# Building four sums of gate weights with six transfers from memory and two copies on the chip

## The chip, the cores and the metric

The kernel runs on one core of one Trainium2 chip. A core has a matrix engine (PE, with its weight loads shown as PEld), a vector engine (DVE), a scalar engine (ACT), a general engine (POOL), a queue engine that issues transfers (SP), and 16 DMA engines that move data between the chip's memory (HBM) and the on-chip buffer. Each engine works through its own instructions in the order in which they were scheduled at build time; an instruction that must wait holds up everything behind it on the same engine. The metric is the device time of one execution in microseconds (us). Before the change the median of three executions is 1417.95 us (1417.14 to 1418.25).

## The reference

The program is a two-layer decoder trunk over 512 tokens of width 1024: a token mixer (Mamba-2 in layer 0, HGRN2 in layer 1), a squared-ReLU MLP, two layer norms and a gated per-layer input. The change lies in the last step of the last layer:

```python
h = layer_norm(DEEPNORM_ALPHA * h + sq_relu_mlp(h, mlp_w1[i], mlp_w2[i]), ln_g[i, 1], ln_b[i, 1])
x = h + jax.nn.sigmoid(h @ ple_w_gate[i]) * (p[i] @ ple_w_proj[i])
```

`ple_w_gate` is a 1024 x 1024 matrix in 32-bit floats.

## The kernel before

**Precision.** Every matrix product in 32-bit precision is made of three: each operand is split into a high part `whi` (a cast on ACT, L113) and a low part `wlo` (value minus high part, on DVE, L116), and `mm3` (L120 to L122) multiplies high by high, high by low and low by high. A weight tile is 128 x 1024 numbers, 512 KB. `unit` loads one into a ring of three buffers named `raw` through SP (L106) and splits it; `split` alone splits a tile that is already on the chip. The rings `whi` and `wlo` hold six tiles each. A `raw` buffer can be loaded again only when the `wlo` subtraction has read it.

**Fewer products by sums.** The second MLP matrix and the last gate use a Strassen-like scheme: seven block products instead of eight, which need four sums of weight blocks, t1 to t4. In the MLP `weight_sums` makes them on DVE from loads into tiles tagged `r`, of which there are eight. In the last gate (`last_gate`) they are made by transfers alone: POOL issues eleven transfers from memory, four plain ones that fill the four tiles with block 4 of the gate's weights, then seven that add another block onto a tile as they write it. Each adding transfer waits until the earlier transfer into its tile has landed. The gate's tiles take over `r` buffers of the last group of MLP sums as those are split and released.

**What stands around it.** The last seven products of the MLP run in the order p1, p7, p6, p4, p5, p2, p3. After p5 (tiles `py`) token chunks 0 and 1 of the result `acc` are complete but for their sums of squares, after p3 chunks 2 and 3. For each chunk DVE adds the product from the PSUM bank into `acc` with a running sum (L372), forms the mean (L213), ACT squares (L215), DVE finishes the variance (L218), scales (L223), ACT takes the root (L219), DVE inverts (L221) and scales and shifts once more (L224). PE then turns the chunk by four transposes at a time (L238), ACT and DVE split the turned half (L242, L243), and the gate's products can read it. PE fills the time between the transposes with `proj`, the product of the per-layer input with `wp` (tiles `pj<-whi,a` and so on).

**What sets the order.** The order on each engine is fixed by a scheduler when the program is built, from the order of the code and the priority of blocks (`tc.high_priority`, where `LEAD` is 100 and `SOON` 40). SP issues the loads in one queue: in the stretch that matters the two tiles of p3 (`raw<-in_w`), then `wp` (`raw<-in_wp`), then four tiles of the gate (`raw<-in_wg`), each as soon as one of the three `raw` buffers is free. POOL has its own queue, and both share the 16 DMA engines.

Of the kernel before, what the change touches and what calls it, by code (L numbers as in the profile page):

```python
# [12 lines left out]
ALU = mybir.AluOpType  # L13
PSUM = bass.MemoryType.PSUM

P = 128
# [12 lines left out]
SOON = 40  # L29
# [15 lines left out]
def trunk(ctx: ExitStack, tc, a):  # L45
    nc = tc.nc
# [21 lines left out]
    def mk(p, shape, tag, dt=F32, **kw):  # L68
        return p.tile(list(shape), dt, tag=tag, name=nm(tag), **kw)

    def f32(t):
        return t.bitcast(F32)
# [16 lines left out]
    def tmp(tag, shape, dt=F32):  # L89
        return mk(phase[0], shape, tag, dt, bufs=phase[2].get(tag, 1))  # L90
# [11 lines left out]
    def unit(src, lead=LEAD, after=None):  # L102
        n = src.shape[1]
        with tc.high_priority(offset=lead):
            raw = mk(raws, [P, 1024], "raw")
            nc.sync.dma_start(raw[:, :n], src)  # L106
        return split(raw[:, :n], lead, after)

    def split(f, lead=LEAD, after=None):
        n = f.shape[1]  # L110
        with tc.high_priority(offset=lead):
            hi = mk(whip, [P, 1024], "whi", F32R)
            nc.scalar.copy(hi[:, :n], f)  # L113
            lo = mk(wlop, [P, 1024], "wlo", F32R)
            with behind(after):
                nc.vector.tensor_sub(lo[:, :n], f, f32(hi[:, :n]))  # L116
        return hi, lo
# [110 lines left out]
    def behind(ins):  # L228
        return tc.issue_after(ins.ins) if ins is not None else nullcontext()
# [91 lines left out]

    def weight_sums(w, lead, eng=nc.vector, after=None):

        t = [[None, None] for _ in range(4)]

        def load(i, u, src):
            t[i][u] = tmp("r", [P, 1024])
            nc.sync.dma_start(t[i][u], src)

        with tc.high_priority(offset=lead):  # L330
            for u in range(2):
                load(0, u, w[0][1][u])
                load(2, u, w[1][1][u])
                with behind(after):
                    eng.tensor_sub(t[2][u], t[2][u], t[0][u])
                load(1, u, w[0][0][u])
                with behind(after):
                    eng.tensor_sub(t[0][u], t[0][u], t[1][u])
                    eng.tensor_add(t[1][u], t[2][u], t[1][u])
            for u in range(2):  # L340
                load(3, u, w[1][0][u])
                with behind(after):
                    eng.tensor_sub(t[3][u], t[3][u], t[1][u])
        return t

    def block_product(w, blk, lead, first, after=None, turns=None, sums=None, low=None):

        t1, t2, t3, t4 = weight_sums(w, lead, after=low)  # L350
        seen = set() if first else {(i, j) for i in range(2) for j in range(2)}
        banks = {}
# [43 lines left out]
    def last_gate(wp, wg, h_s, p_s, kept, turned):  # L396

        t3, t1, t2, t4 = (tmp("r", [P, 1024]) for _ in range(4))
        with tc.high_priority(offset=SOON):
            for t in (t3, t1, t2, t4):  # L400
                nc.gpsimd.dma_start(t, wg[4])
            for t, n in ((t3, 5), (t1, 0), (t2, 5), (t4, 5), (t2, 0), (t4, 0), (t4, 1)):
                nc.gpsimd.dma_start(t, wg[n], accum_op=ALU.add)

        pairs = [mk(b8, [P, 2, 4, 256], "b8", F32R) for _ in range(2)]
        cells = [mk(b8, [P, 4, T], "b8") for _ in range(3)] + [tmp("blk", [P, 4, T])]
# [18 lines left out]
        def direct(i, q):  # L425
            return lambda k, u: (h_s.h(2 * q + k, tok(2 * i + u)), h_s.l(2 * q + k, tok(2 * i + u)))
# [5 lines left out]
        def part(ps, x, w, u, start, stop=True):  # L432
            for k in range(2):
                ks = slice(k * 512, (k + 1) * 512)
                mm3(ps, *x(k, u), w[0][:, ks], w[1][:, ks], start and k == 0, stop and k == 1, skip_group_check=True)
# [21 lines left out]
        pu = unit(wp[0])  # L457
        b11, b21 = unit(wg[0]), unit(wg[1])
        us = [unit(wg[2]), unit(wg[3])]
        t3 = split(t3)  # L460
        turns = turned(1)
        for c in range(NCH):
            ps = bank(psj, "pj")
# [5 lines left out]
        for u in range(2):  # L469
            part(x[u], direct(0, 0), b11, u, True)  # L470
            nc.scalar.copy(cell(4 + u), x[u])

        turns = [turned(2), turned(3)]
        for u in range(2):
# [38 lines left out]
        t2, t4, t1 = split(t2), split(t4), split(t1)  # L513
# [38 lines left out]
    def mlp_and_gate(layer, h_s, last):  # L552
# [54 lines left out]
        if last:  # L607
            return last_gate(a[f"wp_{layer}"], a[f"wg_{layer}"], h_s, p_s, kept, turned)
# [57 lines left out]
    def values4(xs, rows, late):  # L666

        w = [[[a["whvg"][4 * j + 2 * i + u] for u in range(2)] for j in range(2)] for i in range(2)]
        t1, t2, t3, t4 = weight_sums(w, VALUE_SUMS, nc.vector)
        a11, a12, a21, a22 = (rows[i][:, j] for i in range(2) for j in range(2))  # L670
        res = [[mk(w4, [P, 2, T], "ab"[i]) for i in range(2)] for _ in range(2)]
# [292 lines left out]
    for j in range(17):  # L964
# [6 lines left out]
        if pend is not None:  # L971
            i = j - 1
# [485 lines left out]
```

## Time and profile before

| | |
|---|---|
| profiled execution, its own time | 1417.95 us |
| span from first to last instruction in it | 1416.2 us |
| the three timed executions | 1417.95, 1417.14, 1418.25 us |
| busy share of the span | PE 99%, DVE 76%, ACT 54%, POOL 1% |
| moved by DMA | 183.26 MB, 129 GB/s on average |
| POOL's transfers for the gate's sums | 11 of 512 KB, issued from 1305.1 to 1341.6 us |
| matrix engine's mean granted clock | 0.998 of full speed |

All places in time below are us from the first instruction of this execution. The 1.75 us between its span and its own time lie outside the instructions. The profile gives, for each instruction, its start, its length and, in brackets, how long its engine had been idle and what ended that; a chain of waits follows the work back from the last instruction; rows of DMA give the queue's packets, megabytes and the share of the 16 engines' time that they took (q0 is POOL's queue, q1 SP's), or one issue with the time until it landed.

### The profile page before, as it was taken

To read this page: it belongs to the slowest core of one execution; us is meant where nothing else is said; L and a number is where in the kernel's file an instruction comes from. 1 tells how busy PE (TensorE), PEld (TensorE's weight loads), DVE (VectorE), ACT (ScalarE), POOL (GpSimd) and SP (SyncE) were. 2 spreads that over 40 slices of the span, in tenths; PEclk is the share of its full clock that TensorE was granted. 3 is DMA by queue.
4 is the path that set the end of the run, shared out by engine and by line. 5 is a ranking of instruction groups with operands and counts; after the bars stand their busy time and mean duration, and the time that the engine had idled before them with its cause. 6 is when DMAs were issued, how large, how long until landed. Compare 5 with 4: busy or idle time off the path is not lost.

```text
span 1416.2 us, 20365 instructions
## 1 busy us (share of the span) xinstructions
PE 1408.1 (99%) x8001; PEld 1170.3 (83%) x8001; DVE 1070.8 (76%) x1778; ACT 764.3 (54%) x1156; POOL 10.3 (1%) x23
## 2 busy tenths in 40 slices
PE   9999999999999999999999999999999999999998
PEld 7888888888988888888888888888888888888877
DVE  7989587698977667687977577677785767766885
ACT  7766465573454444545546547655554454544573
POOL 0000000000000000000000000000000000000100
PEclk9999999999999999999999999999999999999999
DMA  8333333234334443445621422222163444444921
GB/s 312 136 114 120 107 116 120 75 105 157 141 105 149 135 148 137 146 138 174 208 75 49 141 85 73 76 76 91 58 240 113 153 131 143 132 159 152 233 95 60
DMA packets 50831, 183.26 MB, mean 129 GB/s; under 512 B 5680, under 2 KB 6448, under 8 KB 50608
## 3 DMA queue, kind: packets, MB, share of 16 engines
q1 hardware_dynamic: 49152, 176.20, 36.7%
q0 software_dynamic: 1584, 5.77, 1.9%
q8 instruction: 63, 1.03, 0.3%
q14 instruction: 32, 0.26, 0.1%
HBM read 179.78 MB, written 2.16 MB: 128 GB/s over the span
## 4 chain that ended last, share of the span: by engine, by line
PE 96%; DVE 1%; DMA 1%; ACT 1%; issue 0%; ACTq 0%; DVEq 0%
PE pj L120 24%; PE pj L121 24%; PE pj L122 24%; PE py L120 5%; PE py L121 5%; PE py L122 5%; PE py L900 1%; PE pt L238 1%; PE py L1169 1%; PE pm L917 1%; PE pm L865 1%; DVE wlo L116 1%; DMA raw<-in_w 1%; PE py L1295 1%; PE pt L853 0%; PE py L1297 0%
## 5 line engine op out<-in xcount | busy, mean ns | idle before, releaser
L113 ACT CAST whi<-raw 128x1024 fp32r<-128x1024 f32 x218 | 229.0, 1051 | 332.5 <-PE pj L121 242.3
L120 PE MATMUL pj<-b,whi 128*128 128x512 f32 (+1 forms) x990 | 378.7, 383 | 0.0
L122 PE MATMUL pj<-b,wlo 128*128 128x512 f32 (+1 forms) x990 | 376.7, 381 | 0.0
L121 PE MATMUL pj<-b,whi 128*128 128x512 f32 (+1 forms) x990 | 376.6, 381 | 0.0
L116 DVE TENSOR_TENSOR wlo<-raw,whi 128x1024 fp32r<-128x1024 f32 x218 | 265.6, 1222 | 143.6 <-ACT whi L113 140.0
L121 PEld LDWEIGHTS pj<-b,whi 128*128 128x128 f32 x990 | 186.4, 188 | 34.5 <-issue 0.9
L122 PEld LDWEIGHTS pj<-b,wlo 128*128 128x128 f32 x990 | 186.3, 188 | 34.5
L120 PEld LDWEIGHTS pj<-b,whi 128*128 128x128 f32 x990 | 186.2, 188 | 34.2
L122 PE MATMUL pj<-whi,b 128*128 128x512 f32 x520 | 205.0, 394 | 0.0
L120 PE MATMUL pj<-whi,b 128*128 128x512 f32 x508 | 202.1, 398 | 0.0
L121 PE MATMUL pj<-wlo,b 128*128 128x512 f32 x508 | 199.1, 392 | 0.0
L113 ACT CAST whi<-r 128x1024 fp32r<-128x1024 f32 x76 | 80.0, 1054 | 67.7 <-PE pj L122 38.2
L122 PEld LDWEIGHTS pj<-whi,b 128*128 128x128 f32 x520 | 98.3, 189 | 20.4
L120 PEld LDWEIGHTS pj<-whi,b 128*128 128x128 f32 x508 | 95.5, 188 | 19.0 <-ACT b L1316 0.3
L121 PEld LDWEIGHTS pj<-wlo,b 128*128 128x128 f32 x508 | 95.5, 188 | 18.8 <-issue 0.2
L116 DVE TENSOR_TENSOR wlo<-r,whi 128x1024 fp32r<-128x1024 f32 x76 | 92.6, 1221 | 23.3 <-ACT whi L113 22.7
L122 PE MATMUL py<-whi,b 128*128 128x512 f32 x260 | 101.3, 390 | 0.0
L121 PE MATMUL py<-wlo,b 128*128 128x512 f32 x248 | 96.5, 389 | 0.0
L120 PE MATMUL py<-whi,b 128*128 128x512 f32 x248 | 96.4, 390 | 0.0
L122 PEld LDWEIGHTS py<-whi,b 128*128 128x128 f32 x260 | 48.8, 188 | 10.2
L794 DVE SCALAR_TENSOR_TENSOR cv<-pj,cst,cv 128x509 f32<-128x509 f32 (+2 forms) x66 | 48.9, 746 | 10.4 <-ACT cv L791 9.7
L120 PEld LDWEIGHTS py<-whi,b 128*128 128x128 f32 x248 | 46.6, 188 | 10.1 <-DVE sg L658 0.3
(360 smaller groups left out, 1900.7 us busy)
## 6 DMA issues: line engine op xcount, KB each, us to landing
raw<-in_w SPq DMA_DIRECT2D x112, 512.0 KB, 3.4
r<-in_w SPq DMA_DIRECT2D x64, 512.0 KB, 3.5
raw<-in_wssd SPq DMA_DIRECT2D x36, 512.0 KB, 3.8
a<-csd SPq DMA_DIRECT2D x16, 512.0 KB, 4.1
raw<-in_wso SPq DMA_DIRECT2D x16, 512.0 KB, 3.3
raw<-in_whq SPq DMA_DIRECT2D x16, 512.0 KB, 3.4
raw<-in_wg SPq DMA_DIRECT2D x15, 512.0 KB, 3.9
raw<-in_whvg SPq DMA_DIRECT2D x14, 512.0 KB, 3.4
```

The source lines that it names most:

```text
L113: nc.scalar.copy(hi[:, :n], f)
L116: nc.vector.tensor_sub(lo[:, :n], f, f32(hi[:, :n]))
L120: nc.tensor.matmul(out, sh, mh, start=start, stop=False, **kw)
L121: nc.tensor.matmul(out, sh, ml, start=False, stop=False, **kw)
L122: return nc.tensor.matmul(out, sl, mh, start=False, stop=stop, **kw)
L238: nc.tensor.transpose(pt[:, j * P : (j + 1) * P], src[:, k * P : (k + 1) * P], ident)
L794: nc.vector.scalar_tensor_tensor(cv[:, d:], ps[:, : T - d], convw[:, i, k : k + 1], cv[:, d:], ALU.mult, ALU.add)
L865: nc.tensor.matmul(pst_[:, c * P : (c + 1) * P], btok[:, c, :], xw[:, c].rearrange("p h q -> p (h q)"), start=True, stop=True)
L900: mm = nc.tensor.matmul(yds[0][64 * r : 64 * r + 64, sl], xdt[:, 2 * c + r, :], m[:, r, sl], start=True, stop=True)
L917: mm = nc.tensor.matmul(yo[:, c * P : (c + 1) * P], pv[:, c - 1].rearrange("p h q -> p (h q)"), cm[:, c * P : (c + 1) * P], start=True, st ...
L1169: nc.tensor.matmul(pcs[r][bs, at : at + n], kk[r][:, ts], qs, start=True, stop=True)
L1295: nc.tensor.matmul(po[:, sl], scs[r][:, c, :], v(c, r), start=True, stop=c == 0)
```

## The change

In `last_gate` the list of transfers is new. t3 and t1 are filled with block 4 and get one adding transfer each (blocks 5 and 0). t2 is now a copy of the finished t3 from the on-chip buffer to the on-chip buffer, plus one adding transfer (block 0), and t4 a copy of the finished t2, plus one adding transfer (block 1). The split of t3 moves behind the first block product of the gate and gets the lower priority `SOON`. In `weight_sums` the eight tiles are allocated up front, those of t[2] and t[1] first, instead of one by one as they are loaded.

```diff
     def weight_sums(w, lead, eng=nc.vector, after=None):
 
-        t = [[None, None] for _ in range(4)]
+        t = [None] * 4
+        for i in (2, 1, 3, 0):
+            t[i] = [tmp("r", [P, 1024]) for _ in range(2)]
 
         def load(i, u, src):
-            t[i][u] = tmp("r", [P, 1024])
             nc.sync.dma_start(t[i][u], src)
...
         t3, t1, t2, t4 = (tmp("r", [P, 1024]) for _ in range(4))
         with tc.high_priority(offset=SOON):
-            for t in (t3, t1, t2, t4):
-                nc.gpsimd.dma_start(t, wg[4])
-            for t, n in ((t3, 5), (t1, 0), (t2, 5), (t4, 5), (t2, 0), (t4, 0), (t4, 1)):
-                nc.gpsimd.dma_start(t, wg[n], accum_op=ALU.add)
+            nc.gpsimd.dma_start(t3, wg[4])
+            nc.gpsimd.dma_start(t1, wg[4])
+            nc.gpsimd.dma_start(t3, wg[5], accum_op=ALU.add)
+            nc.gpsimd.dma_start(t1, wg[0], accum_op=ALU.add)
+            nc.gpsimd.dma_start(t2, t3)
+            nc.gpsimd.dma_start(t2, wg[0], accum_op=ALU.add)
+            nc.gpsimd.dma_start(t4, t2)
+            nc.gpsimd.dma_start(t4, wg[1], accum_op=ALU.add)
...
         us = [unit(wg[2]), unit(wg[3])]
-        t3 = split(t3)
         turns = turned(1)
...
             part(x[u], direct(0, 0), b11, u, True)
             nc.scalar.copy(cell(4 + u), x[u])
+        t3 = split(t3, SOON)
 
```

POOL, the gate's transfers, before. `r_11783` is t3, `r_11784` t1, `r_11785` t2 and `r_11786` t4; L401 fills, L403 adds.

```order
L401 DMA r_11783<-in_wg 128x1024
L403 DMA r_11783<-in_wg 128x1024
L401 DMA r_11784<-in_wg 128x1024
L401 DMA r_11785<-in_wg 128x1024
L403 DMA r_11784<-in_wg 128x1024
L401 DMA r_11786<-in_wg 128x1024
L403 DMA r_11785<-in_wg 128x1024
L403 DMA r_11786<-in_wg 128x1024
L403 DMA r_11785<-in_wg 128x1024
L403 DMA r_11786<-in_wg 128x1024 x2
```

The same place in the changed program (L404, L406 and L408 add; L405 and L407 copy on the chip).

```order
L401 DMA r_11783<-in_wg 128x1024
L403 DMA r_11783<-in_wg 128x1024
L402 DMA r_11784<-in_wg 128x1024
L405 DMA r_11785<-r_11783 128x1024
L404 DMA r_11784<-in_wg 128x1024
L406 DMA r_11785<-in_wg 128x1024
L407 DMA r_11786<-r_11785 128x1024
L408 DMA r_11786<-in_wg 128x1024
```

Eleven transfers became eight, seven adding ones became four, and from the second row on each link of t3, t2, t4 stands behind the one before.

DVE, the norm's end for chunks 0 and 1 and what follows it, before. `wlo_11832` is the low part of the gate's block 3, `wlo_11836` that of t3; `pt_11726` and `pt_11741` are the two turned halves of chunk 0, `lnmv` the means of chunks 2 and 3.

```order
L224 SCALAR_TENSOR_TENSOR acc_99<-acc_99,lnrs_11658,b_11418 128x1024
L116 TENSOR_TENSOR wlo_11832<-raw_11828,whi_11830 128x1024
L243 TENSOR_TENSOR b_1772_11423<-pt_11726,b_1770_11421 128x4x128
L116 TENSOR_TENSOR wlo_11836<-r_11783,whi_11834 128x1024
L372 ISA acc_99,lnsum_11425<-py_1792_11468,acc_99 128x512
L372 ISA lnsum_11425 128x1
L372 ISA acc_99,lnsum_11425<-py_1793_11469,acc_99 128x512
L372 ISA lnsum_11425 128x1
L243 TENSOR_TENSOR b_1773_11424<-pt_11741,b_1771_11422 128x4x128
L213 TENSOR_SCALAR lnmv_11755<-lnsum_11425 128x1
L213 TENSOR_SCALAR lnmv_11769<-lnsum_11425 128x1
```

The same place in the changed program.

```order
L224 SCALAR_TENSOR_TENSOR acc_99<-acc_99,lnrs_11658,b_11418 128x1024
L116 TENSOR_TENSOR wlo_11829<-raw_11825,whi_11827 128x1024
L243 TENSOR_TENSOR b_1772_11423<-pt_11726,b_1770_11421 128x4x128
L373 ISA acc_99,lnsum_11425<-py_1792_11468,acc_99 128x512
L373 ISA lnsum_11425 128x1
L373 ISA acc_99,lnsum_11425<-py_1793_11469,acc_99 128x512
L373 ISA lnsum_11425 128x1
L213 TENSOR_SCALAR lnmv_11755<-lnsum_11425 128x1
L213 TENSOR_SCALAR lnmv_11769<-lnsum_11425 128x1
L116 TENSOR_TENSOR wlo_11896<-r_11783,whi_11894 128x1024
L243 TENSOR_TENSOR b_1773_11424<-pt_11741,b_1771_11422 128x4x128
```

The low part of t3 stands behind the sums and means of chunks 2 and 3 instead of ahead of them. Ahead of these rows no engine but POOL has another order than before, and SP's order is the same throughout.

## The prediction

> **What bounds the kernel now.** I read the page's busy shares first, then who waited for whom on PE, then the chain of waits in order of time where the longest wait lies, then the DMA view of that stretch.
>
> ```profile
> PE 1408.1 (99%) x8001; PEld 1170.3 (83%) x8001; DVE 1070.8 (76%) x1778; ACT 764.3 (54%) x1156; POOL 10.3 (1%) x23
> PE pt L238 <- DVE acc L224: 2.8, 1, 2.8
> ...
> PE pj L120 <- ACT b L509: 0.2, 1, 0.2
> ```
>
> PE is the bound: the change leaves every matmul as it is, so it can act only on PE's waits and on PE's clock. One wait is large: 2.8 us for the layer norm of chunk 0 (L224). It costs more than its length:
>
> ```profile
> 1344.68 0.39 PE L120 MATMUL py<-whi,blk 128*128 128x512 f32 x1
> ...
> 1349.89 0.39 PE L122 MATMUL py<-whi,blk 128*128 128x512 f32 x1
> 1353.11 1.11 PE L238 MATMUL pt<-cst,acc 128*128 128x128 f32 x4 [2.83 <-DVE acc L224]
> 1353.87 0.77 PE L120 MATMUL pj<-whi,a 128*128 128x512 f32 x1
> ...
> 1359.14 0.40 PE L120 MATMUL pj<-whi,a 128*128 128x512 f32 x1
> 1353.00:1359.20 6.20, 6.09 (x17) 4.92 (x18) 5.33 (x9) 1.18 (x2) 0.00 (x0) 0.51 0.42 147
> 1359.20:1365.40 6.20, 6.20 (x33) 5.07 (x32) 2.98 (x6) 5.21 (x12) 0.00 (x0) 1.00 0.00 0
> ```
>
> After the wait PE runs at a granted clock of 0.51 for 6.2 us, then at 1.00 again. The 13 matmuls that start from 1353.87 to 1359.14 (two chunks of six and one) stand 5.27 / 12 = 0.44 us apart, p3's 24 from 1344.68 to 1349.89 stand 5.21 / 23 = 0.23 apart: 12 x 0.21 = 2.5 us, and about 0.4 for the four transposes ahead of them (0.76 us at the half clock). The wait and its slow clock are worth 2.8 + 2.9 = 5.7 us. The chain says who is late:
>
> ```profile
> 1329.66 7.82 DMA raw<-in_w
> ...
> 1337.57 1.06 ACT whi L113
> ...
> 1338.66 1.23 DVE wlo L116
> ...
> 1340.53 0.23 DVE lnmv L213
> ...
> 1343.82 4.92 DMA raw<-in_wg
> ...
> 1351.85 1.21 DVE acc L224
> ...
> 1353.11 1.11 PE pt L238 x4
> ```
>
> The norm stands on DVE and ACT in line with splits of weight tiles, and those wait for loads. p3's two tiles, issued at 1327.37 and 1329.66, took 7.8 us each, `wp` behind them 9.7:
>
> ```profile
> 1327.37 2.61 SPq L106 DMA_DIRECT2D raw<-in_w  x2
> raw<-in_w SPq DMA_DIRECT2D x1, 512.0 KB, 7.8
> 1330.90 0.33 SPq L106 DMA_DIRECT2D raw<-in_wp  x1
> raw<-in_wp SPq DMA_DIRECT2D x1, 512.0 KB, 9.7
> 1335.32 1.05 ACT L113 CAST whi<-raw 128x1024 fp32r<-128x1024 f32 x1 [5.70 <-DMA raw<-in_w]
> 1336.40 1.23 DVE L116 TENSOR_TENSOR wlo<-raw,whi 128x1024 fp32r<-128x1024 f32 x1 [4.32 <-ACT whi L113]
> 1336.29 0.39 PE L122 MATMUL py<-whi,b 128*128 128x512 f32 x1
> 1339.80 0.68 DVE L372 CUSTOM_DVE_ANT_0 acc<-py,acc 128x512 f32<-128x512 f32 x1
> ```
>
> DVE stood idle for 4.3 us, and so took PE's product for chunk 0 at 1339.80 although PE had begun its last matmul at 1336.29. An ordinary load takes 3.2 us; these were slow because POOL's adding transfers shared the DMA engines:
>
> ```profile
> 1327.00:1349.00 22.00, 22.00 (x99) 18.22 (x98) 15.56 (x27) 10.28 (x16) 2.61 (x3) 1.00 0.95 258
> q0 software_dynamic: 1440, 5.24, 66.0%
> q1 hardware_dynamic: 923, 3.39, 24.2%
> q0 software_dynamic: 144, 0.52, 39.1%
> r<-in_wg POOLq DMA_DIRECT2D x1, 512.0 KB, 3.8
> r<-in_wg POOLq DMA_DIRECT2D x1, 512.0 KB, 5.4
> raw<-in_wg SPq DMA_DIRECT2D x1, 512.0 KB, 3.2
> raw<-in_wg SPq DMA_DIRECT2D x1, 512.0 KB, 4.9
> 1341.61 0.87 POOL L403 DMA_DIRECT2D r<-in_wg  x1 [8.14 <-DMA r<-in_wg]
> ```
>
> From 1327 to 1349 the DMA engines are 0.95 busy. The first two queue rows cover 1309 to 1347.1 (38.1 us), the third 1305 to 1309.2, where POOL's first fill is alone. So a plain transfer of POOL costs 39.1% of 4.2 = 1.6 us of all 16 engines; the ten others took 25.1 us, three of them plain, which leaves (25.1 - 4.9) / 7 = 2.9 us for an adding one. The issue rows: the fill at 1305.13 lands after 3.8 us, the first adding one after 5.4; a load of SP takes 3.2 alone (1355.41) and 4.9 beside an adding transfer (1337.65).
>
> **The change, part by part.** *Transfers.* Three adding transfers go (3 x 2.9 = 8.7 us of the engines), and two fills become copies on the chip. No row shows a copy from chip to chip. Its bounds are the plain fill (1.6 us of the engines, landing after 3.8) and the adding one (2.9; 5.4), which also reads the chip; I take the fill, because like it the copy moves every byte once and computes nothing. By the Trainium skill's formula in "DMA: Bandwidth & Descriptors", section "Anatomy of one DMA" (a fixed 2.0 us and bytes over 436 GB/s), a 512 KB copy would land after an estimated 3.2 us; the sum would be the same.
>
> *When they run.* t3 is filled at 1305.13 as before, lands at 1308.9, its adding transfer at about 1314.6 (1309.26 + 5.4). Behind it stand in line copy, add, copy, add: with a fill's 3.8 and an add's 5.4, and about 2 us for t1's two transfers and a norm load sharing, the copy into t2 lands near 1319.5, t2 is done near 1325.5, the copy into t4 near 1329.5, t4 near 1336. With copies at 5.4 it is 1339. Now the last one is only issued at 1341.61. So when p3's loads are issued (1327.37, 1329.66) they meet one POOL transfer at a time, where now they meet parts of three adding ones. I take 4.5 and 4.9 us for them, by the row with one neighbour; bounds 3.2 (alone) and 7.8 (no gain).
>
> *What follows from the loads.* First tile at 1331.9: high part on ACT, low part on DVE (1.06 and 1.23 us, as in the chain), both done by 1334.3. Second at 1334.6: done by 1336.95. PE's product for chunk 0 is ready by 1336.7 (1336.29 + 0.39), so L372 runs at 1336.95, 2.85 us earlier than now, and the mean at 1337.7. From there to PE's transposes now take 1353.11 - 1340.53 = 12.6 us, nearly all of it work in line on DVE and ACT; if it holds, PE begins them at 1350.3, just after its last matmul of p3 lets go (1349.89 + 0.23 = 1350.12). The links that could break it: `wp` must land by about 1338.6, 2.8 us ahead of its use now (third in SP's line, it now lands at 1330.90 + 9.7 = 1340.6), the gate's third tile, 4.92 us from 1343.82, is issued 2.8 us earlier and meets no POOL transfer, and the high parts wait for PE to free a buffer of the `whi` ring, for the third tile at p2's end, about 1344.9 (p3's first matmul starts at 1344.68). These may add up to 0.8 us; I take 0.4, so a rest of about 0.5 us of the 2.8.
>
> *Clock.* With a rest of 0.5 us I take the clock to stay at 1.00, since the wait of 0.2 us at L509 leaves it there; 2.9 us gained. Bounds: nothing, and 2.9.
>
> *t3's split moves* (1.06 us of ACT, 1.23 of DVE): it stands behind the sums of chunks 2 and 3, which helps their norm by about 1.1 us on DVE, and its first reader on PE starts at 1380.82, so its lateness is free. POOL's extra waiting is free too: behind the last transfer nothing stands on POOL, and the first reader of the other sums is ACT's split of t2 at 1367.11, 40 us after t2 is due, t4's about 2 us behind it:
>
> ```profile
> 1367.11 1.06 ACT L113 CAST whi<-r 128x1024 fp32r<-128x1024 f32 x1
> 1380.82 0.39 PE L120 MATMUL pj<-whi,b 128*128 128x512 f32 x1
> 1360.63 0.69 DVE L243 TENSOR_TENSOR b<-pt,b 128x512 fp32r<-128x512 f32 x1 [2.29 <-ACT b L242]
> 1363.15 0.69 DVE L243 TENSOR_TENSOR b<-pt,b 128x512 fp32r<-128x512 f32 x1 [1.59 <-ACT b L242]
> 1367.82 2.48 DVE L224 SCALAR_TENSOR_TENSOR acc<-acc,lnrs,b 128x1024 f32<-128x1024 f32 x2
> 1369.45 0.60 PE L238 MATMUL pt<-cst,acc 128*128 128x128 f32 x4
> ```
>
> The allocation up front in `weight_sums` costs nothing: every sum stays in the buffer pattern of the group before, and SP's order is unchanged.
>
> *What is late next.* PE arrives earlier at the transposes of chunk 2 than their norm was asked for so far. PE needs 1369.45 - 1353.11 - 2.5 = 13.8 us from one to the other at full clock: 1364.4 after a start at 1350.6. DVE needed 1367.82 - 1351.85 = 16.0 us from chunk 0's L224 to the start of chunk 2's, with 2.29 + 1.59 = 3.9 us of idling for casts of turned halves that now come earlier too. From 1349.0, and with the 1.2 us of L224 itself, that is 1362.3 to 1366.2. So this costs 0 to 1.8 us; I take 0.6, as PE's earlier transposes should end most of that idling.
>
> *The sum* against the profiled execution's own 1417.95 us, which is also the median: -2.3 (wait), -2.9 (clock), +0.6 (next wait) = -4.6, or **1413.3 us**; with the bounds 1412.2 (no rest, no next wait) to 1414.8 (a rest of 0.8, a next wait of 1.8). 0.2%, 2.8 us, is about what a measurement of this kernel can tell from no change, so faster begins below 1415.1.
>
> **The rivals.** *The clock falls all the same.* One case of a fall, at 2.83 us, does not tell how short a wait still triggers it; the 0.2 us wait speaks against, a rest near 1 us is untested. Then only 2.3 - 0.6 = 1.7 us are gained: 1416.2. The Trainium skill ("TensorE: Matmul & The Clock Gate", section "Part 1: The HAM clock gate") puts the fall after an idle window of about 3.4 us; the row shows it after 2.83, so that threshold is not borne out here, and nothing in my sum uses it.
>
> *The loads stay slow.* If copies cost the engines far more than adding transfers, p3's loads meet as much traffic as now, and chunk 0's norm stays late: 1417.95 less the 0.2 at L509 is 1417.7. Against it: eight transfers for eleven, and one at a time.
>
> *The wait moves.* DVE and ACT have so little room behind 1350 that PE idles at chunk 2 or 3 long enough to lose the clock there: -5.2 + 1.8 + 2.9, 1417.4. For it: DVE's path behind 1349 has only those 3.9 us of idling to give. Against: the waits would be several short ones.
>
> *Slower: t2 comes late.* t2 and t4 now hang on one chain of five transfers. ACT meets t2's split in line at about 1367.11 - 4.6 = 1362.5, ahead of casts that PE waits for, so if the chain needs longer than the 48 us from 1314.6 to there, every us is lost on PE, and the clock with it. That takes copies of over 18 us each; with 25 us, t4 comes at 1314.6 + 25 + 5.4 + 25 + 5.4 = 1375.4, some 11 us after ACT would meet it: 1413.3 + 11 + 2.9 = 1427. Against it: of the rows above the slowest landing is 9.7 us.
>
> **How the numbers follow.** The forecast 0.62, the clock 0.14, slow loads 0.10, the moved wait 0.08, slower 0.06. The predicted time is the likeliest, 1413.3 us. The range goes from 1411.5 (the low bound, and the waits at chunk 2 better than thought) to 1417.5, which takes in the clock, the moved wait and half of the slow loads. Faster 0.64 (the forecast and a little of the clock's case), same 0.29, slower 0.07.
>
> **What would show it.** Right: POOL's last landing near 1336; p3's loads at 4 to 5 us; ACT's wait for them 5.70 shrunk below 3; L224 near 1349; PE's wait at `pt` under 1 us; a granted clock of 1.00 from 1350 on. Wrong: a copy over 5.4 us, p3's loads over 6 us, or a clock near 0.5 behind a short wait.

## The result, and the profile after

The changed kernel takes 1412.37 us (median of six runs, 1411.49 to 1415.41) against 1418.14 us for the kernel before: ratio 0.9961, 95% interval 0.9949 to 0.9974. Two later sets of runs gave 1413.00 us (0.9968, 0.9956 to 0.9980) and 1412.45 us (0.9957, 0.9945 to 0.9970). It is faster by about 0.4%, 4 to 6 us; 1413.3 us was predicted.

The first profile of the changed kernel is that of its slowest run, 1415.41 us (span 1413.6). From its page the busy shares and POOL's queue:

```profile
PE 1406.7 (100%) x8001; PEld 1168.7 (83%) x8001; DVE 1070.2 (76%) x1778; ACT 764.0 (54%) x1156; POOL 7.7 (1%) x20
q0 software_dynamic: 1152, 4.19, 1.3%
```

POOL moves 4.19 MB instead of the 5.76 of before (5.24 and 0.52 in the two rows shown there), three transfers less. Who waited for whom on PE, as us in total, times, longest:

```profile
PE pt L238 <- DVE acc L224: 1.1, 1, 1.1
PE py L120 <- DVE lnsum L373: 0.9, 1, 0.9
```

The wait for chunk 0's norm has shrunk from 2.8 to 1.1 us. The windows that answer to those shown of before (PE's busy time is the second figure, the granted clock the third from the end) show no slow clock behind it:

```profile
1353.60:1359.80 6.20, 6.18 (x31) 4.99 (x32) 6.10 (x11) 3.11 (x8) 0.00 (x0) 1.00 0.48 159
1359.80:1366.00 6.20, 6.20 (x32) 4.80 (x31) 5.95 (x10) 6.20 (x15) 0.00 (x0) 1.00 0.00 0
```

The second row of the waits is new, and it stands at 703.77 us, in the layer before, where the list plays no part. Of the 13 profiles of this document it appears in three: here, with the allocation alone (0.8 us) and with t1 late (0.3 us). All three have the new allocation, but so have five profiles without the wait, and the runs of the allocation alone are not slower; whether it hangs on the allocation or is chance is open. Together with 1.0 us more in the first 50 us, it makes this one execution late by 2.2 us long before the gate. A second and a third profile of the changed kernel are not late there. So the time is best split at three marks that the timeline of PE gives: the start of p3's last matmul, of chunk 0's transposes, and of the last matmul of all.

| us | before, 1st profile | before, 2nd | changed, 1st | changed, 2nd | changed, 3rd |
|---|---|---|---|---|---|
| p3's last matmul starts at | 1349.89 | 1350.08 | 1352.12 | 1350.08 | 1349.99 |
| from there to the transposes | 3.22 | 4.07 | 1.50 | 0.47 | 0.46 |
| from the transposes to the last matmul | 58.94 | 57.52 | 55.90 | 55.85 | 55.90 |
| from the last matmul to the end | 4.13 | 4.12 | 4.12 | 4.11 | 4.11 |
| span | 1416.2 | 1415.8 | 1413.6 | 1410.5 | 1410.5 |

Of the second profiles the rows themselves, first before, then changed (start, length, engine, line, operation):

```profile
1350.08 0.39 PE L122 MATMUL py<-whi,blk 128*128 128x512 f32 x1
1354.15 1.11 PE L238 MATMUL pt<-cst,acc 128*128 128x128 f32 x4 [3.69 <-DVE acc L224]
...
1411.67 0.28 PE L122 MATMUL pm<-a,b 128*128 128x256 f32 x1
```

```profile
1350.08 0.39 PE L122 MATMUL py<-whi,blk 128*128 128x512 f32 x1
1350.55 0.66 PE L238 MATMUL pt<-cst,acc 128*128 128x128 f32 x4
...
1406.39 0.28 PE L122 MATMUL pm<-a,b 128*128 128x256 f32 x1
```

The two are level to 0.01 us up to p3's end. Then 5.3 us are gained: 3.60 ahead of the transposes and 1.67 behind them. In the changed kernel's second profile the bracket is gone, PE no longer waits there at all.

The loads of that profile, of the issues that start from 1327 to 1338 (KB each, median us to landing):

```profile
raw<-in_w SPq DMA_DIRECT2D x2, 512.0 KB, 4.4
r<-r POOLq DMA_DIRECT2D x1, 512.0 KB, 5.6
raw<-in_wp SPq DMA_DIRECT2D x1, 512.0 KB, 4.6
```

p3's two tiles, 7.8 us each before, land after 4.2 and 4.6 us beside the copy into t4, and `wp` after 4.6 instead of 9.7.

What let the norm come earlier is seen on ACT, in its timeline of the same profile: the high parts of p3's two tiles and of the gate's first.

```profile
1332.83 1.05 ACT L113 CAST whi<-raw 128x1024 fp32r<-128x1024 f32 x1 [3.02 <-PE pj L122]
1334.49 1.05 ACT L113 CAST whi<-raw 128x1024 fp32r<-128x1024 f32 x1 [0.60 <-DMA raw<-in_w]
...
1340.71 1.06 ACT L113 CAST whi<-raw 128x1024 fp32r<-128x1024 f32 x1 [0.35 <-DMA raw<-in_wg]
```

Before, ACT idled 5.70 us for the load of p3's first tile. Now that load is there in time, and the idle time ends with PE, which frees a buffer of the `whi` ring; loads account for 0.60 and 0.35 us. DVE's rows show the rest, the mean of chunk 0 and the norm's end:

```profile
1337.64 0.21 DVE L213 TENSOR_SCALAR lnmv<-lnsum 128x1 f32<-128x1 f32 x1
...
1349.21 2.48 DVE L224 SCALAR_TENSOR_TENSOR acc<-acc,lnrs,b 128x1024 f32<-128x1024 f32 x2
```

Both stand where the prediction put them (1337.7 and near 1349).

In the first profile 1.1 us were left. Its chain of waits names the piece:

```profile
1337.20 6.49 DMA raw<-in_wg
1343.79 1.06 ACT whi L113
1344.88 1.22 DVE wlo L116
...
1352.37 1.21 DVE acc L224
1353.62 0.66 PE pt L238 x4
```

The gate's first tile took 6.5 us, beside t4's adding transfer, which in that execution took 6.9 us to land; in the second profile they took 5.5 and 5.3.

### The profile page after: what moved, and what is told of

Read it like the earlier page. It is cut to its first block, busy times and chain, and to the rows that moved or that the text cites. A ratio compares the mean times of both kernels' runs of the same rounds, so it can differ in the third digit from the quotient of the medians.

```text
span 1413.6 us, 20360 instructions
## 1 busy us (share of the span) xinstructions
PE 1406.7 (100%) x8001; PEld 1168.7 (83%) x8001; DVE 1070.2 (76%) x1778; ACT 764.0 (54%) x1156; POOL 7.7 (1%) x20
## 3 DMA queue, kind: packets, MB, share of 16 engines
q0 software_dynamic: 1152, 4.19, 1.3%
## 4 chain that ended last, share of the span: by engine, by line
PE 96%; DVE 2%; DMA 1%; issue 0%; ACT 0%; ACTq 0%; DVEq 0%
PE pj L120 25%; PE pj L121 24%; PE pj L122 24%; PE py L120 5%; PE py L122 5%; PE py L121 5%; PE py L905 1%; DVE wlo L116 1%; PE pt L238 1%; PE py L1174 1%; PE pm L870 1%; PE pm L922 1%; PE py L1300 1%; PE pt L858 0%; DMA raw<-in_wg 0%; DMA raw<-in_w 0%
```

## The experiments

All times are medians. Every kernel below keeps the order of instructions on PE, DVE and ACT of one of the two kernels, row by row; what differs is only what its edit says. "Wait at pt" is PE's wait for chunk 0's norm in one profile.

| kernel | runs | median us | ratio to before, 95% interval | wait at pt |
|---|---|---|---|---|
| list alone | 5 | 1412.96 | 0.9966 (0.9954 to 0.9978) | 0.4 |
| split alone | 11 | 1418.00 | 0.9998 (0.9990 to 1.0007) | 3.9 |
| old eleven, in line | 12 | 1414.18 | 0.9978 (0.9969 to 0.9986) | 1.7 |
| t1 late | 7 | 1413.91 | 0.9970 (0.9959 to 0.9981) | 0.7 |
| eight, apart | 6 | 1413.18 | 0.9968 (0.9956 to 0.9980) | none |
| fills alone | 6 | 1412.31 | 0.9963 (0.9950 to 0.9977) | none |
| changed, 2nd | 6 | 1413.00 | 0.9968 (0.9956 to 0.9980) | none |
| before, 2nd | 1 | 1417.56 | | 3.7 |
| allocation alone | 11 | 1418.90 | 1.0001 (0.9992 to 1.0010) | 4.3 |
| list alone, 2nd | 5 | 1412.39 | 0.9956 (0.9944 to 0.9969) | 0.3 |
| changed, 3rd | 5 | 1412.45 | 0.9957 (0.9945 to 0.9970) | none |

The first four were run together on one chip (before: 1418.59), so were the next four (before: 1417.33) and the last three (before: 1418.56).

**The list alone.** To the kernel before:

```diff
-            for t in (t3, t1, t2, t4):
-                nc.gpsimd.dma_start(t, wg[4])
-            for t, n in ((t3, 5), (t1, 0), (t2, 5), (t4, 5), (t2, 0), (t4, 0), (t4, 1)):
-                nc.gpsimd.dma_start(t, wg[n], accum_op=ALU.add)
+            nc.gpsimd.dma_start(t3, wg[4])
...
+            nc.gpsimd.dma_start(t4, wg[1], accum_op=ALU.add)
```

> The kernel before with the new list of eight transfers alone: t3's split stays at its old place and weight_sums allocates as before. My theory (the lateness comes from p3's loads beside the adding transfers, so the list carries the gain): p3's loads take 4 to 5 us, PE's wait at pt falls from 2.8 to about 1.1 us as in the changed kernel, the clock stays at 1.00 behind it, and the time is 1412 to 1414 us; about 1 us of it may be lost at the norm of chunk 2 or 3, since t3's split still stands ahead of it on DVE. Rival (the gain comes from the place of t3's split, which changes the order on PE, ACT and DVE behind chunk 0): the time stays at 1416.5 us or more.

The time, the loads (4.45 and 4.70 us) and the clock are as my theory said; the wait, 0.4 us, was shorter than the 1.1 expected. The rival falls.

**The split alone.** To the kernel before:

```diff
-        t3 = split(t3)
...
             part(x[u], direct(0, 0), b11, u, True)
             nc.scalar.copy(cell(4 + u), x[u])
+        t3 = split(t3, SOON)
```

> The kernel before with only t3's split moved behind the loop over x. My theory: the wait at pt stands ahead of everything that this moves, so 2.8 us of wait and the half clock behind it stay, and the time is 1417 to 1418 us (0 to 1.1 us less, from DVE's split that no longer stands ahead of the sums of chunks 2 and 3). Rival (the split's place carries the gain): 1414 us or less.

No difference that the runs can tell (0.9998). PE, DVE and ACT have the changed kernel's order here, yet the wait stays, and the issues that start from 1327 to 1338 (KB each, median us to landing) are slow as before:

```profile
1354.35 1.11 PE L238 MATMUL pt<-cst,acc 128*128 128x128 f32 x4 [3.92 <-DVE acc L224]
```

```profile
raw<-in_w SPq DMA_DIRECT2D x2, 512.0 KB, 7.3
r<-in_wg POOLq DMA_DIRECT2D x2, 512.0 KB, 8.6
raw<-in_wp SPq DMA_DIRECT2D x1, 512.0 KB, 9.9
```

**The allocation alone.** To the kernel before: the eight `r` tiles allocated up front, as in the change.

```diff
-        t = [[None, None] for _ in range(4)]
+        t = [None] * 4
+        for i in (2, 1, 3, 0):
+            t[i] = [tmp("r", [P, 1024]) for _ in range(2)]
...
-            t[i][u] = tmp("r", [P, 1024])
```

> The kernel before with only the allocation of the eight r tiles in weight_sums moved up front. My theory: nothing, since every engine's order stays and every sum keeps the same pattern of buffers: within 1 us of the kernel before, a wait at pt of 2.5 to 4 us. Rival (the gate's tiles come into buffers that are free earlier, so POOL's chain starts earlier): POOL's first transfer is issued ahead of 1305, its last before 1339, and the time falls by 2 us or more.

Ratio 1.0001; POOL's first transfer at 1306.03, its last issued at 1341.97. So of the three edits the list carries the whole gain.

**How the list does it: number or crowding?** Two kernels take the two apart. The first keeps all eleven old transfers in the changed kernel, but queues them sum by sum:

```diff
+            last = None
+            for t, ns in ((t3, (5,)), (t1, (0,)), (t2, (5, 0)), (t4, (5, 0, 1))):
+                for n in (None, *ns):
+                    with behind(last):
+                        if n is None:
+                            last = nc.gpsimd.dma_start(t, wg[4])
+                        else:
+                            last = nc.gpsimd.dma_start(t, wg[n], accum_op=ALU.add)
```

> The changed kernel with the old eleven transfers (four fills, seven adding ones), but queued sum by sum: t3's two, t1's two, t2's three, t4's four, so that an adding transfer of a sum meets at most the fill or the adding one of the next sum and never three adding ones at a time. Theory A (how many adding transfers run at once is what made p3's loads slow): p3's loads take 5 to 6 us, the wait at pt is 1 to 2 us, the time 1412.5 to 1414.5 us. Theory B (the bytes that are still to be moved count: 25 us of all 16 engines have to fit in somewhere): p3's loads still take about 7 us, the last landing is 1350 or later, the gate's first loads get slower still, the wait at pt is 2.5 us or more and the clock falls: 1417 us or more.

The old eleven without the crowd give 4.4 of the 5.6 us that the list alone gave on that chip. POOL's own rows (idle time before in brackets) show where the transfers went:

```profile
1329.77 0.86 POOL L408 DMA_DIRECT2D r<-in_wg  x1 [5.02 <-DMA r<-in_wg]
1330.35 0.83 POOL L406 DMA_DIRECT2D r<-in_wg  x1
1340.07 0.87 POOL L408 DMA_DIRECT2D r<-in_wg  x1 [8.89 <-DMA r<-in_wg]
1345.84 0.87 POOL L408 DMA_DIRECT2D r<-in_wg  x1 [4.90 <-DMA r<-in_wg]
1352.10 0.87 POOL L408 DMA_DIRECT2D r<-in_wg  x1 [5.39 <-DMA r<-in_wg]
```

From 1329.4, when t2's first adding transfer has landed, to 1340 only t2's last one and t4's fill run beside the loads, where before parts of three adding ones did; t4's three come after, and its last lands at 1359.81, still ahead of its split. p3's loads took 3.7 and 4.6 us. `wp` took 8.2, and the gate's third tile, in which the chain of waits ends here, 6.1 beside t4's first adding transfer; 1.7 us of wait are left. Theory A's time and wait hold; of theory B only the late last landing came true.

The second takes the changed kernel's number, four adding and four plain transfers, and drops the chain. Left out are t2's block 5 and t4's blocks 5 and 0.

```diff
+            for t in (t3, t1, t2, t4):
+                nc.gpsimd.dma_start(t, wg[4])
+            for t, n in ((t3, 5), (t1, 0), (t2, 0), (t4, 1)):
+                nc.gpsimd.dma_start(t, wg[n], accum_op=ALU.add)
```

> The changed kernel with eight transfers that don't hang on one another: four fills from memory and one adding transfer for each sum (t2 lacks wg[5], t4 lacks wg[5] and wg[0]), queued as the scheduler puts them. As many transfers and adding transfers as in the change, but free to run two or three at a time. Theory A (fewer adding transfers are enough): POOL's last landing comes before 1336, p3's loads take 4 to 5 us, the wait at pt is 0.4 to 1.1 us and the time 1411.5 to 1412.6 us, that of the change. Theory B (the chain of the change matters, since it keeps the transfers one at a time): p3's loads take 6 us or more, the wait at pt is 1.7 us or more, 1414 us.

1413.18 against 1413.00 us for the changed kernel on the same chip, no wait at pt, POOL's last landing at 1331.8. The time expected (1411.5 to 1412.6) was too low for both, and p3's first load, still beside an adding transfer, took 5.6 us (4 to 5 expected) without harm; the second took 4.7. So the chain is not needed, and the smaller number is not needed for most of the gain: what both do is to leave fewer adding transfers for the 13 us in which p3's tiles and `wp` are loaded.

**What was left of the wait.** In the changed kernel t1's fill moves to SP's queue behind `wp[1]`, and its adding transfer to the end of POOL's:

```diff
             nc.gpsimd.dma_start(t3, wg[4])
-            nc.gpsimd.dma_start(t1, wg[4])
             nc.gpsimd.dma_start(t3, wg[5], accum_op=ALU.add)
-            nc.gpsimd.dma_start(t1, wg[0], accum_op=ALU.add)
...
+            load = nc.sync.dma_start(raw, wp[1])
...
+            with behind(load):
+                nc.sync.dma_start(t1, wg[4])
+            with behind(last):
+                nc.gpsimd.dma_start(t1, wg[0], accum_op=ALU.add)
```

> The changed kernel with t1's two transfers taken out of the chain: t1's fill goes on SP's queue behind wp[1], its adding transfer is POOL's last; t3, t2 and t4 come first, with nothing of t1 beside them. My theory (what is left of the wait at pt, 1.1 us, is the gate's first tile, whose load took 6.5 us beside t4's adding transfer): t4's adding transfer lands 4 to 5 us earlier than in the changed kernel, the gate's first tile takes 5 us or less, ACT's wait of 1.30 us for it goes, the wait at pt is 0.3 us or less, and the time is about 1 us under the changed kernel's: 1411.3 us. Rival (the wait is set by PE, which frees the buffers of the high parts: ACT waits 3.02 us for one at 1334.86): the wait at pt stays at 0.8 us or more and the time at 1412.4.

Both were wrong on the time: 1413.91, above the changed kernel's three medians and above the list alone on the same chip (1412.96). t4's adding transfer was issued early, 2.6 us behind p3's first load (6.0 in the second profile of the change), but did not land early, nor did `wp` beside it (issues that start from 1330 to 1341):

```profile
r<-in_wg POOLq DMA_DIRECT2D x1, 512.0 KB, 9.3
raw<-in_wp SPq DMA_DIRECT2D x1, 512.0 KB, 8.5
```

The late tile became `wp` in place of the gate's first, and 0.7 us of wait stayed. A further 0.4 us went at the end: the span closes 4.56 us after the last matmul here, against 4.11. As to what was left in the kernels with the list, the theory fits the profiles: the gate's first tile landed 8.4 us ahead of p3's last matmul where the wait was 1.1, 9.1 and 9.2 us ahead in the two of the list alone (0.4 and 0.3), and 9.5 us ahead in the second of the change, where there was none.

**The floor.** The changed kernel with the four fills alone; all adding transfers and copies are left out.

```diff
             for t in (t3, t1, t2, t4):
                 nc.gpsimd.dma_start(t, wg[4])
```

> The changed kernel with the four fills alone: all adding transfers and copies are left out, so the sums are wg[4] each. The floor of what lighter traffic can give. Theory A (what is left of the wait at pt, 0.4 to 1.1 us, comes from loads beside POOL's transfers): p3's loads, wp and the gate's tiles take 3.2 to 4.5 us, the wait at pt is 0.2 us or less, the time 1411 us. Theory B (a floor set by the work in line on DVE and ACT, and by the buffers of the high parts that PE frees): the wait at pt stays at 0.4 us or more, and the time within 0.6 us of the changed kernel's 1412.4.

Theory A's wait holds (none; the loads from 1327 to 1338 took 3.3 to 4.5 us, medians below), its time does not: 1412.31 us is the time that theory B gave, 0.7 under the changed kernel on that chip. So lighter traffic has about 0.7 us left to give, which six runs each, spread over 1.6 and 1.2 us, barely tell from nothing.

```profile
raw<-in_w SPq DMA_DIRECT2D x2, 512.0 KB, 3.4
raw<-in_wg SPq DMA_DIRECT2D x2, 512.0 KB, 3.9
raw<-in_wp SPq DMA_DIRECT2D x1, 512.0 KB, 4.4
```

**Second profiles of both kernels**, unchanged:

> The changed kernel once more, for a second profile on the chip of these experiments. If its first profile was late by chance ahead of 1300 us (1.0 us by 50 us, 1.3 us at about 709 with a 0.9 us wait at py for L373, where nothing was changed), this one starts p3 within 0.5 us of the kernel before (1344.7) and shows no wait at py; if the change caused it, p3 starts at 1346.9 again. The wait at pt is 0.4 to 1.1 us, the time 1411.8 to 1413.0 us.

It starts p3 at 1344.87 (1350.08 less the 5.21 us of its 24 matmuls) and shows no wait at `py` for L373: the lateness doesn't come with every execution of the change. The wait at pt is gone rather than 0.4 to 1.1.

> The kernel before once more, for a second profile. If the clock is judged on a grid of 3.41 us that runs on its own, as the stretches of 6.83 us (before) and 3.41 us (only the split moved) suggest, the slow stretch is again one or two times 3.41 us, begins 0 to 3.4 us after PE's last matmul of p3, and costs 1.1 or 3.0 us; if it hangs on the length of the wait alone, a wait near 2.8 us gives 6.8 us again and one near 3.9 gives 3.4. The wait at pt is 2.5 to 4 us, the time 1416.5 to 1419.5 us.

The time and the wait are as expected. For the clock, windows cut at its changes, in the first and in the second profile of before (us, then PE's busy time; the granted clock third from the end):

```profile
1348.90:1352.31 3.41, 1.38 (x7) 0.80 (x5) 3.36 (x7) 3.22 (x5) 0.00 (x0) 1.00 0.43 167
1352.31:1355.72 3.41, 2.61 (x8) 2.23 (x9) 3.41 (x4) 0.59 (x1) 0.00 (x0) 0.50 0.50 169
1355.72:1359.14 3.42, 3.42 (x10) 2.63 (x8) 2.61 (x6) 0.59 (x1) 0.00 (x0) 0.50 0.43 153
```

```profile
1350.25:1353.65 3.40, 0.22 (x1) 0.00 (x0) 2.70 (x6) 2.93 (x5) 0.00 (x0) 1.00 0.60 192
1353.65:1357.07 3.42, 2.92 (x9) 2.53 (x10) 3.42 (x5) 0.59 (x2) 0.00 (x0) 0.50 0.32 119
1357.07:1360.48 3.41, 3.41 (x18) 2.81 (x18) 2.56 (x6) 1.44 (x3) 0.00 (x0) 1.00 0.43 154
```

The slow stretch is two steps of 3.41 us after a wait of 2.83 and one step after 3.69. The split alone (wait 3.92) had one step too, the allocation alone (4.27) two. Waits of 2.83, 3.69, 3.92 and 4.27 us with two, one, one and two steps follow no rule by which a longer wait has more steps, or fewer; a grid fits all four.

**The place of t3's split.**

> The kernel before with the new list alone once more, on one chip with the whole change. From its first profile the old place of t3's split costs 0.4 us behind the transposes of chunk 0 (56.30 us from there to the last matmul, 55.85 and 55.90 in the changed kernel, with a 0.2 us wait for L509's cast): if that is so, 56.2 to 56.4 us again and a median 0.2 to 0.8 us above the changed kernel's. If it was chance: within 0.1 us of 55.9, and the medians equal.

> The changed kernel a third time, for comparison on the same chip: a wait at pt of 0 to 1.1 us, the clock at 1.00, 1411.8 to 1413.2 us, ratio to the kernel before 0.9955 to 0.9975.

56.29 us from the transposes to the last matmul again, so the old place does cost 0.4 us there, with the same short wait (L513 is L509 in this kernel):

```profile
PE pt L238 <- DVE acc L224: 0.3, 1, 0.3
PE pj L120 <- ACT b L513: 0.2, 1, 0.2
```

The medians, 1412.39 and 1412.45, do not show it: five runs each, spread over 1.2 and 1.0 us, can't settle 0.4 us. In these two profiles p3's last matmul starts 0.4 us earlier in the list alone (1349.60 against 1349.99), which hides it.

## Why the prediction was right

**The bound and the late thing.** PE's wait at `pt`, the slow clock behind it, and p3's loads beside adding transfers as their cause: the list alone, the split alone and the allocation alone settle that the list does it, the old eleven in line and the fills alone that it is the adding transfers beside the loads.

**The transfers.** I gave a copy a fill's cost, 1.6 us of all 16 engines, and an adding transfer 2.9. The kernel with t1 late has both alone on POOL's queue, in the DMA views from 1316 to 1320.6 (the copy into t2, beside a norm load of SP) and from 1321 to 1326.4 (t2's adding transfer, beside nothing):

```profile
q0 software_dynamic: 144, 0.52, 29.8%
```

```profile
q0 software_dynamic: 144, 0.52, 61.3%
```

That is 29.8% of 4.6 = 1.4 us for a copy and 61.3% of 5.4 = 3.3 us for an adding one. The copies landed later than the 3.8 us I took, in the three profiles of the change after 4.9 to 6.1 and once 3.1. So one of my signs of being wrong, a copy over 5.4 us, came true; the second profile, with copies of 6.1 and 5.6 us, has no wait at pt all the same. The copies ran beside loads and t1's adding transfer; with t1 late they took 4.7 and 3.5 us, which fits that as the cause. POOL's last landing was at 1338.8 in the second profile and 1338.7 in the third, where I had 1336 (1339 was the bound with slower copies; the steps that I listed, with the 2 us of sharing, add up to 1335), and p3's loads took 4.2 and 4.6 us in the second (4.5 and 4.9 predicted).

**The rest of the wait.** I took 0.5 us. The five profiles with the new list show 1.1, 0.4, 0.3 and twice nothing. The mean and L224 came where they were put. The `whi` ring did set the pace, as feared, but for p3's first tile and not the third: ACT's 3.02 us ending with PE, without harm.

**The clock.** It stays at 1.00 behind the 1.1 us wait, and behind 1.72 us with the old eleven in line. The rival in which it falls all the same is out for the rests seen here. Its worth was mis-sized as a constant: 2.9 us was one case of two. Against 56.30 us with the old place of the split, the first profile of before loses 58.94 - 56.30 = 2.6 us to it and the second 57.52 - 56.30 = 1.2. The wait makes up for most of it the other way, 2.8 and 3.7.

**What is late next.** This term failed: 0.6 us (0 to 1.8) was to be lost at chunk 2. The stretch from the transposes to the last matmul takes 55.85 to 55.90 us in all three profiles of the change and 55.69 with fills alone, so at most 0.2 is lost. The move of t3's split, which the sum left at nothing, has a part in that: with the split at its old place and the new list the stretch takes 56.3. Also, the clock's worth behind the transposes went into this term with 2.5 us and into the sum with 2.9. Without the 0.6 the sum is 2.3 + 2.9 = 5.2 us, against 5.3 between the second profiles and 5.8 between the first medians. Between the second profiles the two terms are right in sum alone: the wait gave 1.3 us more, the clock and what follows 1.2 less.

**The other rivals.** The loads did not stay slow, the wait did not move, and t2 was far from late.

## What to carry to other kernels

When a load that a chain hangs on is slow, ask what else is on the DMA engines in just those microseconds: moving or spreading that traffic gained 4.4 of 5.6 us here without a byte less. A short wait of the matrix engine may be worth more than its length when it makes the clock fall, as waits of 2.8 us and more did here and one of 1.7 did not, so remove the whole of it or shorten it. And take a second profile before explaining one or two microseconds: here 2.2 us of lateness and a 1.1 us wait in the first profile were gone in the next.

## What the runs showed of the hardware

The granted clock changes in steps of 3.41 us, and the points of change move against the program from one execution to the next (1352.31 and 1353.65 in the same kernel). It fell at the end of a step in which PE was busy for 1.38 us, and one of 0.22, and with the allocation alone after one of 1.44; it did not fall in the kernel with the old eleven in line after a step with 1.97 us (the steps are counted on from the clock's first rise, at 6.17 us there):

```profile
1351.01:1354.43 3.42, 1.97 (x11) 1.73 (x12) 3.42 (x5) 1.40 (x2) 0.87 (x1) 1.00 0.95 283
1354.43:1357.84 3.41, 3.41 (x18) 2.64 (x17) 3.41 (x9) 1.72 (x4) 0.00 (x0) 1.00 0.96 201
```

Nor did it in the second profile of the changed kernel after the step in which its matmuls end, with 1.80 us (first rise at 5.40 us); the step behind is still at 1.00:

```profile
1404.87:1408.28 3.41, 1.80 (x14) 1.56 (x12) 1.61 (x4) 0.60 (x1) 0.00 (x0) 1.00 0.11 38
1408.28:1411.69 3.41, 0.00 (x0) 0.00 (x0) 0.00 (x0) 0.00 (x0) 0.00 (x0) 1.00 0.12 39
```

It came back after steps with 2.92 us of work and 2.81 (the split alone), and not after one with 2.61. The Trainium skill ("TensorE: Matmul & The Clock Gate", section "Part 1: The HAM clock gate") gives a window of 3413 ns that runs freely; the stretches agree with that. The same section lets the clock fall after an idle window; here a window in which PE worked for 40% of the time was enough. Where the threshold lies between 1.44 and 1.80 us is open. By these rows (an estimate) a wait under 3.41 - 1.80 = 1.6 us keeps the clock wherever it falls on the grid, if PE is busy around it; the 1.72 us of the old eleven in line lay across two steps, and might have lost it inside one.

An adding transfer can slow down together with a load beside it far beyond their shares: with t1 late, t4's and `wp` took 9.3 and 8.5 us, in the second profile of the change 5.3 and 4.6, in the third 8.5 and 7.9. The order of issue goes with it. `wp` was issued at 1331.80, 1331.09 and 1331.00; t4's adding transfer with t1 late at 1330.88, and in the second and the third profile of the change at

```profile
1333.53 0.87 POOL L408 DMA_DIRECT2D r<-in_wg  x1 [5.48 <-DMA r<-r]
1330.24 0.87 POOL L408 DMA_DIRECT2D r<-in_wg  x1 [3.02 <-DMA r<-r]
```

Where the adding transfer went 0.8 or 0.9 us ahead of `wp`, both were slow; where it came 2.4 us behind, as also in the first profile of the change and 2.6 behind in both of the list alone, `wp` took 4.6 to 4.8 us. A shorter chain on POOL can so put an adding transfer ahead of a load, as with t1 late. That the order is the cause is not shown: no run changed it alone.
